# Seven of eleven column pairs of an up projection with seven combined products for eight in a quarter of their K range

## The chip, the cores and the metric

The kernel runs on one core of one Trainium2 chip. The metric is the device time of one launch in microseconds (us), as the median of several runs. One more execution was recorded by the hardware profiler; its page and its trace are what is read here. The engines are named as in the profile: PE is TensorE's matmul, PEld its weight load, DVE is VectorE, ACT is ScalarE, POOL is GpSimd, SP is SyncE. POOL and SP do little but issue transfers here.

## The reference

One decoder layer for 256 tokens of width 2048. The part that the change touches is the gated MLP at its end:

```python
h = rms_norm(x, ln2[l])
u = causal_dwconv(h @ w_up[l], ffn_conv[l], ffn_conv_bias[l])
u_gate, u_val = jnp.split(u, 2, axis=-1)
x = x + (jax.nn.silu(u_gate) * u_val) @ w_down[l]
```

`w_up` is 2048 x 11264: 5632 gate columns and 5632 value columns. `w_down` is 5632 x 2048.

## The kernel before

**Products of three.** All large products take fp32 inputs apart into a high part in the fp32r format and a low part, the rest. ACT casts the high part, DVE subtracts it from the source (`split`, lines 104 and 101 of the profile), and TensorE multiplies high by high, high by low and low by high (`main_mm`, line 93). The weights come as raw blocks of 128 x 2048 fp32, 1 MB each (`fetch`, line 116), into `wraw`, which has four buffers; POOL's queue asks for those of the MLP. A block is split in two halves of 1024 columns. The parts go to a ring of four places (`wh` and `wl`), so a half can be cast when TensorE has finished with the half four before it.

**The up projection** (`ps_up`) takes 22 column blocks of 512 columns, a gate block and then its value block, so 11 column pairs. K has 16 blocks of 128 rows. `by_token` works through one column block with four raw blocks; a raw block holds four K-blocks. The activations `h2`, high and low, are the stationary side (128 x 128), the weights the moving side (128 x 512). A column block has two token halves, two PSUM banks, and 16 x 2 x 3 = 96 products, a pair 192, the projection 2112. A half of 1024 columns holds two K-blocks and feeds 12 products.

**Behind each column block** ACT scales the two banks into `ut` (line 1003), and `convolved` runs in the background: DVE transposes 32 x 32 blocks (line 470), 16 small transfers of SP's queue put the blocks in place (`uc<-xt`, line 475), and after a pause four channels follow one by one, each a scaled copy on ACT (line 956), two steps on DVE (line 958), and for a value block the product with the gate (line 975) into `acts`. The gate block ends with a Silu (line 980). The background advances by one step for every eight wide products (`tick`, `EVERY`); `wait(12)` is the pause of twelve steps between the transfers and the convolution. Another background task turns the residual `x1` in four parts (`residual_turned`).

**The down projection** (`pd`) follows without a break, on the same ring with three more places. Some of its blocks already use seven combined products for eight (`seven`, `folds`): DVE adds quarters of the raw block (line 1049), and sums on PSUM are put together at the end (lines 1075 to 1083).

**What sets the order.** Each engine executes its own list in order. The tile framework puts the lists together while the program is built, from the order in the code, priorities and `issue_after`; which instruction stands before which can be listed from the built program. A wait of one instruction holds everything behind it on that engine.

## Time and profile before

| | |
|---|---|
| Median of three runs | 1395.56 us (1395.29 to 1396.97) |
| Profiled execution | 1401.47 us, span 1399.7 us |
| Up projection, first to last product | 696.3 to 1161.8 us |
| Busy in the span | PE 1386.3, PEld 1203.2, DVE 1036.1, ACT 794.3, POOL 128.5 us |
| Mean granted TensorE clock | 0.997 of full speed |

The profile gives, for each group of instructions, the line, the engine, the operation, what it writes and reads by the program's names, how often, the busy time and the mean duration, then the idle time of the engine before it and what ended that. `wl<-wraw,wh` is a low part on DVE, `wh<-wraw` a cast on ACT, `ah` and `al` are the parts of the activations of the down projection. Products on TensorE overlap, so the distance of their starts tells more than their duration. In the views by window, the columns are the busy microseconds and the number of instructions of each engine, the granted clock, the busy share of the DMA engines and GB/s.

### The profile page before, as it was taken

Reading aid. Unit: us, or ns where it says so; the run is one execution under the profiler, and the core shown is the slowest. Engines: PE = TensorE matmul, PEld = TensorE weight load, DVE = VectorE, ACT = ScalarE, POOL = GpSimd, SP = SyncE. Lnnn points to the kernel's source line nnn. Section 1 sums busy time; section 2 is a strip of 40 time slices with the busy share of each in tenths; the row PEclk is TensorE's granted clock in tenths of the full one; section 3 lists DMA queues with packets and bytes.
Section 4 is the critical chain, followed back from the end, with each engine's and each line's share of the span. In section 5 each row is a group of like instructions: output and inputs, shape, how many; then the busy total and the mean of one; then the engine's idle time right before and its main releaser. Section 6 shows DMA issues by size and latency. Waiting matters only on the chain.

```text
span 1399.7 us, 19586 instructions
## 1 busy us (share of the span) xinstructions
PE 1386.3 (99%) x7222; PEld 1203.2 (86%) x7222; DVE 1036.1 (74%) x1544; ACT 794.3 (57%) x987; POOL 128.5 (9%) x204
## 2 busy tenths in 40 slices
PE   9999999999999999999999999999999999999997
PEld 8998899888888888889888888888888888888886
DVE  7988886987664446767757676676676676999994
ACT  6765455645466544445546555555555566666763
POOL 0021000200001100001201011010110110101110
PEclk9999999999999999999999999999999999999999
DMA  9566554567546555776567888888888777556562
GB/s 366 182 214 214 210 197 132 189 194 262 197 133 214 210 189 183 243 260 216 192 209 223 241 218 236 237 222 235 230 227 235 220 227 229 200 186 231 179 246 72
DMA packets 204672, 297.40 MB, mean 212 GB/s; under 512 B 167096, under 2 KB 169536, under 8 KB 172064
## 3 DMA queue, kind: packets, MB, share of 16 engines
q1 hardware_dynamic: 165648, 150.31, 35.5%
q0 software_dynamic: 21088, 142.17, 29.8%
q10 hardware_dynamic: 17840, 3.67, 1.3%
q8 instruction: 56, 0.92, 0.3%
q14 instruction: 40, 0.33, 0.1%
HBM read 273.48 MB, written 3.15 MB: 198 GB/s over the span
## 4 chain that ended last, share of the span: by engine, by line
PE 95%; DMA 3%; DVE 1%; issue 0%; SPq 0%; ACT 0%; DVEq 0%; ACTq 0%
PE ps_up L93 33%; PE pd L93 14%; PE ps_gate L93 11%; PE ps_gdn L93 9%; PE ps_wo L93 6%; PE ps_br L93 6%; PE ps_moba L93 5%; PE ps_v L93 3%; PE ps_z L93 3%; DMA uc<-xt 1%; PE g L81 1%; PE ps_gdn L262 1%; DMA dT<-X 0%; DMA xs<-in_xw 0%; DMA TL<-dT 0%
## 5 line engine op out<-in xcount | busy, mean ns | idle before, releaser
L101 DVE TENSOR_TENSOR wl<-wraw,wh 128x1024 fp32r<-128x1024 f32 (+1 forms) x476 | 576.1, 1215 | 288.7 <-ACT wh L104 282.5
L104 ACT CAST wh<-wraw 128x1024 fp32r<-128x1024 f32 (+1 forms) x476 | 491.7, 1038 | 457.3 <-PE ps_up L93 168.2
L93 PE MATMUL ps_up<-wh,h 128*128 128x512 f32 x1408 | 422.8, 380 | 0.2 <-DVE x L918 0.2
L93 PEld LDWEIGHTS ps_up<-wh,h 128*128 128x128 f32 x1408 | 264.2, 188 | 46.0 <-issue 0.6
L93 PE MATMUL ps_up<-wl,h 128*128 128x512 f32 x704 | 267.6, 380 | 0.0
L93 PE MATMUL ps_gate<-wh,hc 128*128 128x512 f32 x512 | 155.4, 382 | 0.0
L93 PEld LDWEIGHTS ps_up<-wl,h 128*128 128x128 f32 x704 | 132.2, 188 | 22.7
L93 PE MATMUL ps_gdn<-hc,wh 128*128 128x256 f32 x720 | 124.2, 276 | 0.0
L93 PEld LDWEIGHTS ps_gate<-wh,hc 128*128 128x128 f32 x512 | 95.8, 188 | 16.3
L93 PEld LDWEIGHTS ps_gdn<-hc,wh 128*128 128x128 f32 x720 | 108.5, 188 | 1.3 <-issue 0.6
L93 PE MATMUL ps_gate<-wl,hc 128*128 128x512 f32 x256 | 97.9, 383 | 0.0
L93 PE MATMUL ps_gdn<-hc,wl 128*128 128x256 f32 x360 | 97.9, 275 | 0.0
L93 PE MATMUL ps_wo<-mc,wh 128*128 128x512 f32 x256 | 85.6, 379 | 0.0
L116 POOL DMA_DIRECT2D wraw<-in_w_up x88 | 46.9, 532 | 413.7 <-DVE wl L101 413.7
L93 PE MATMUL pd<-tt,ah 128*128 128x512 f32 x282 | 82.6, 381 | 0.0
L93 PE MATMUL ps_moba<-wh,hc 128*128 128x512 f32 x256 | 77.1, 381 | 0.0
L93 PE MATMUL ps_wo<-mc,wl 128*128 128x256 f32 x256 | 70.5, 276 | 0.0
L93 PEld LDWEIGHTS ps_gdn<-hc,wl 128*128 128x128 f32 x360 | 67.1, 188 | 0.3
L104 ACT CAST tt<-wraw 128x1024 fp32r<-128x1024 f32 x46 | 47.4, 1045 | 30.7 <-PE pd L93 25.0
L93 PE MATMUL pd<-wh,ah 128*128 128x512 f32 x156 | 59.7, 384 | 1.7 <-ACT ah L104 1.7
L93 PEld LDWEIGHTS pd<-tt,ah 128*128 128x128 f32 x282 | 53.2, 189 | 9.3
L93 PE MATMUL pd<-wh,al 128*128 128x512 f32 x156 | 59.3, 385 | 0.7 <-DVE al L101 0.7
(445 smaller groups left out, 1980.4 us busy)
## 6 DMA issues: line engine op xcount, KB each, us to landing
wraw<-in_w_up POOLq DMA_DIRECT2D x88, 1024.0 KB, 5.7
wraw<-in_w_dn POOLq DMA_DIRECT2D x44, 1024.0 KB, 5.9
wraw<-in_w_gate SPq DMA_DIRECT2D x32, 1024.0 KB, 4.9
wraw<-in_w_gdn SPq DMA_DIRECT2D x22, 1024.0 KB, 4.9
wraw<-in_w_moba SPq DMA_DIRECT2D x16, 1024.0 KB, 6.2
wraw<-in_w_o SPq DMA_DIRECT2D x16, 1024.0 KB, 5.7
uc<-xt SPq DMA_DIRECT2D x352, 32.0 KB, 4.6
wraw<-in_w_z SPq DMA_DIRECT2D x8, 1024.0 KB, 7.1
```

What stands on the lines that cost most here:

```text
L81: pe.matmul(ps, a, b, start=(start and i == 0), stop=(stop and i == n - 1), **kw)
L93: r = pe.matmul(ps, a, b, start=start, stop=stop, skip_group_check=True)
L101: return (eng or dve).tensor_tensor(lo, src, hi.bitcast(F32), op=ALU.subtract)
L104: casts.append(act.copy(hi, src))
L116: fetcher[0].dma_start(raw[:, :n], src)
L262: pe.matmul(ps_q0[:, b], wq[:, j, b * P:(b + 1) * P], xs[:, j], start=(j == b == 0), stop=False, skip_group_check=True)
```

## The change

The column pairs 1 to 7 (`UPS`) take their first four K-blocks together: with the two token halves, the two column blocks (gate and value) and two groups of two K-blocks, the first quarter of K is a 2 x 2 by 2 x 2 block product. Instead of eight block products of six matmuls, `fewer` does seven of six (Strassen's scheme in Winograd's form): 42 matmuls for 48.

- Four combinations of the activations are built once, in the background of the first pair (`combinations`, `forms`).
- For each changed pair, DVE makes four sums over the raw blocks (`t1`, `r11`, `t2` twice), seven halves are split where four were, ACT copies the first product out of PSUM (`m1`), and DVE folds five sums of 512 columns (`fold_v`, `fold_y`, and three that are written back to PSUM).
- Six of the seven stand ahead of the gate block's other three raw blocks; the seventh (`rest`) and the last two folds stand behind them. The background takes no step while the six are put out (`paused`).
- The host puts the first quarter of gate and value columns into two raw blocks by K-block (`up_blocks`). The first lies in a `wraw` buffer as before; the second is asked for by the code a column block earlier and lies in a part of `acts` that is still free (`spare(28, 8)`). In POOL's list of the built program its fetch stands directly behind the first's.
- All pairs run through `one_side`, with four PSUM banks to a pair instead of two to a column block; pairs take turns on all eight banks (`four_banks`).
- Background buffers: `xt` has two buffers, which the residual's turning shares; the gate `sgt` has one instead of two. The last column block's pause is 15 steps instead of 12.

```diff
+UPS = (1, 2, 3, 4, 5, 6, 7)
...
-    spent = [0]
+    spent, paused = [0], [False]
...
-        if spent[0] >= EVERY:
+        if spent[0] >= EVERY and not paused[0]:
...
-    def fetch(src, n=2048):
-        raw = wpool.tile([P, 2048], F32, name="wraw", tag="wraw", bufs=4)
-        fetcher[0].dma_start(raw[:, :n], src)
-        return raw
+    def fetch(src, raw=None):
+        if raw is None:
+            raw = wpool.tile([P, 2048], F32, name="wraw", tag="wraw", bufs=4)
+        fetcher[0].dma_start(raw, src)
+        return [raw[:, 1024 * h:1024 * h + 1024] for h in range(2)]
...
-    turned_ring = [3]
+    turned_ring = [(3 + len(UPS)) % 4]
...
-                        ub.tile([P, 8, P], F32, name="xt"), sp, 4, 1)
-        yield from wait(12)
+                        ub.tile([P, 8, P], F32, name="xt", bufs=2), sp, 4, 1)
+        yield from wait(12 if n < NF // 2 - 1 else 15)
         if not val:
-            gates[c] = ub.tile([P, 4, T], F32, name="sgt", bufs=2)
...
+    forms = [[b.tile([P, 2 * T + 64], F32R, name=t, tag=t)[:, 8:8 + 2 * T] for t in ("ah", "al")] for _ in range(2)]
+
+    def combinations():
+        raw = acts[:, 40:44, :]
+        sums = acts[:, 36:40, :].rearrange("p k t -> p (k t)").rearrange("p (f j t) -> p f j t", f=4, t=P)
+        for k in range(4):
+            act.activation(raw[:, k, :], x1[:, k, :], AF.Identity, scale=ln2v[:, k:k + 1])
+        a11, a12, a21, a22 = (raw[:, e::2, i * P:i * P + P] for i in range(2) for e in range(2))
+        s7, s5, s6, s3 = (sums[:, n] for n in range(4))
+        yield
+        dve.tensor_tensor(s7, a11, a21, op=ALU.subtract)
+        dve.tensor_tensor(s5, a21, a22, op=ALU.subtract)
+        yield
+        dve.tensor_tensor(s6, a22, s7, op=ALU.add)
+        dve.tensor_tensor(s3, a12, s6, op=ALU.subtract)
+        for n, (hi, lo) in enumerate(forms):
+            yield
+            split(hi, lo, sums[:, 2 * n:2 * n + 2].rearrange("p f j t -> p (f j t)"))
+
+    def part(src):
+        w = parts(60)
+        lows.append(split(*w, src))
+        return w
+
+    def products(w, them):
+        for bank, a, n, start in them:
+            for y_, x_ in ((0, 0), (0, 1), (1, 0)):
+                main_mm(fours(bank), a[x_], fours(half(w[y_], n, 512)), start and y_ + x_ == 0, False)
+
...
+    def fewer(ps, raw1, raw2):
+        c11, c12, c21, c22 = ps
+        fold_v, fold_y = spare(40, 2), spare(42, 2)
+
+        def of(k, i):
+            return [h_of(k + 2 * j, i) for j in range(2)]
+
+        def pair_of(bank, a, w, start=False):
+            products(w, [(bank, a[j], j, start and j == 0) for j in range(2)])
+
+        s7, s5, s6, s3 = ([combined(n, j) for j in range(2)] for n in range(4))
+
+        def add(to, one, other, op=ALU.add):
+            dve.tensor_tensor(to, one, other, op=op)
+
+        (r10, r11), (r20, r21) = raw1, raw2
+        t1 = ub.tile([P, 1024], F32, name="t1")
+        t2 = spare(36, 4)
+        add(t1, r10, r11)
+        add(r11, r11, r21)
+        add(t2, t1, r21)
+        pair_of(c11, of(0, 0), part(r10), True)
+        m1 = b.tile([P, 4 * P], F32, name="m1", tag="S", bufs=1)
+        act.copy(m1, c11)
+        pair_of(c22, s6, part(t2), True)
+        add(fold_v, c22, m1, ALU.subtract)
+        pair_of(c21, s7, part(r11), True)
+        add(t2, t2, r20)
+        add(fold_y, c21, fold_v, ALU.subtract)
+        add(c21, c21, fold_v, ALU.subtract)
+        pair_of(c12, s5, part(t1), True)
+        pair_of(c11, of(1, 0), part(r20))
+        pair_of(c21, of(1, 1), part(t2))
+
+        def rest():
+            with tc.issue_after(lows[-1].ins):
+                add(c22, c12, fold_y, ALU.subtract)
+                add(c12, c12, fold_v)
+            pair_of(c12, s3, part(r21))
+
+        return rest
+
+    def one_side(ps, c, side, q0, to=4):
+        for q in range(q0, to):
+            raw = fetch(w_up[8 * c + 4 * side + q])
+            for h in range(2):
+                w = part(raw[h])
+                k = 4 * q + 2 * h
+                products(w, [(ps[2 * i + side], h_of(k + n, i), n, k + n == 0) for i in range(2) for n in range(2)])
+
+    def spare(ch, n):
+        return acts[:, ch:ch + n, :].rearrange("p k t -> p (k t)")
+
...
+    def four_banks(name):
+        turned[0] ^= 1
+        t = [mmt(name).rearrange("p a b -> p (a b)") for _ in range(4 if turned[0] else 2)]
+        return [t[n] for n in (0, 2, 1, 3)] if turned[0] else [sdt(name) for _ in range(2)] + t
+
+    bg.append(combinations())
+    bg.append(residual_turned())
+    for c in range(NU):
+        ps = four_banks("ps_up")
+        rest = None
+        if c in UPS:
+            paused[0] = True
+            rest = fewer(ps, fetch(w_up[8 * c]), second)
+            paused[0] = False
+        one_side(ps, c, 0, c in UPS)
+        evicted(c, ps, 0)
+        if rest:
+            rest()
+        if c + 1 in UPS:
+            second = fetch(w_up[8 * c + 12], spare(28, 8))
+        one_side(ps, c, 1, c in UPS, 4 - (c == NU - 1))
+        if c < NU - 1:
+            evicted(c, ps, 1)
+    pd = four_banks("pd")
+    banks = [[0, 1, 2, 3], [4, 5, 6, 7]]
+    residual_in(0)
+    one_side(ps, NU - 1, 1, 3)
+    evicted(NU - 1, ps, 1)
+    pd += four_banks("pd")
...
+    def up_blocks(w):
+        w = w.reshape(KD, P, 2, NF // 4, 512).transpose(3, 1, 0, 2, 4)
+        w = np.stack([w[:, :, k:k + 4, n] for n in range(2) for k in range(0, KD, 4)], axis=1)
+        for c in UPS:
+            w[c, [0, 4]] = np.stack([np.concatenate([w[c, n, :, e::2] for n in (0, 4)], axis=1) for e in range(2)])
+        return w.reshape(-1, P, 2048)
```

**On TensorE**, where a new pair begins: a number behind a name is a buffer's. Before, the first raw block of a column block:

```order
L93 MATMUL ps_up_6905<-wh_61,h2_5401 128x4x32x4 x2
L93 MATMUL ps_up_6905<-wl_62,h2_5401 128x4x32x4
L93 MATMUL ps_up_6905<-wh_61,h2_5401 128x4x32x4 x2
L93 MATMUL ps_up_6905<-wl_62,h2_5401 128x4x32x4
L93 MATMUL ps_up_6906<-wh_61,h2_5401 128x4x32x4 x2
L93 MATMUL ps_up_6906<-wl_62,h2_5401 128x4x32x4
```

Now, the first two of the seven combined products of pair 2 (6760 and 6763 are two of its banks; `ah_6145` and `al_6146` are a combination of the activations):

```order
L94 MATMUL ps_up_6760<-wh_61,h2_5401 128x4x32x4 x2
L94 MATMUL ps_up_6760<-wl_62,h2_5401 128x4x32x4
L94 MATMUL ps_up_6760<-wh_61,h2_5401 128x4x32x4 x2
L94 MATMUL ps_up_6760<-wl_62,h2_5401 128x4x32x4
L94 MATMUL ps_up_6763<-wh_61,ah_6145 128x4x32x4
L94 MATMUL ps_up_6763<-wh_61,al_6146 128x4x32x4
L94 MATMUL ps_up_6763<-wl_62,ah_6145 128x4x32x4
L94 MATMUL ps_up_6763<-wh_61,ah_6145 128x4x32x4
L94 MATMUL ps_up_6763<-wh_61,al_6146 128x4x32x4
L94 MATMUL ps_up_6763<-wl_62,ah_6145 128x4x32x4
```

A split half now serves one bank with six products, where it served two banks with twelve.

**On DVE**, at the same place. Before, low parts of two raw blocks with the convolution between them:

```order
L101 TENSOR_TENSOR wl_62<-wraw_8033,wh_61 128x1024
L975 TENSOR_TENSOR acts_6142<-sgt_7820,cvf_8014 128x256
L958 SCALAR_TENSOR_TENSOR cvf_8028<-uc_7751,ffv_5500,cvf_8028 128x255
L958 SCALAR_TENSOR_TENSOR cvf_8028<-uc_7751,ffv_5500,cvf_8028 128x254
L101 TENSOR_TENSOR wl_62<-wraw_8033,wh_61 128x1024
L975 TENSOR_TENSOR acts_6142<-sgt_7820,cvf_8028 128x256
L101 TENSOR_TENSOR wl_62<-wraw_8069,wh_61 128x1024 x2
```

Now, pair 5 from its third split half (`wraw_7783`, r11) to the first half of the next raw block (`wraw_7843`); L1037 are the new sums and folds:

```order
L1037 TENSOR_TENSOR acts_6142<-acts_6142 128x1024
L102 TENSOR_TENSOR wl_62<-wraw_7783,wh_61 128x1024
L102 TENSOR_TENSOR wl_62<-t1_7785,wh_61 128x1024
L102 TENSOR_TENSOR wl_62<-acts_6142,wh_61 128x1024
L1037 TENSOR_TENSOR acts_6142<-ps_up_7780,m1_7797 128x512
L102 TENSOR_TENSOR wl_62<-acts_6142,wh_61 128x1024
L1037 TENSOR_TENSOR acts_6142<-ps_up_7779,acts_6142 128x512
L1037 TENSOR_TENSOR ps_up_7779<-ps_up_7779,acts_6142 128x512
L102 TENSOR_TENSOR wl_62<-wraw_7843,wh_61 128x1024
L960 SCALAR_TENSOR_TENSOR cvf_7849<-uc_7514,ffv_5500,cvf_7849 128x255
L472 STREAM_TRANSPOSE xt_7855<-ut_7776 128x1024
L960 SCALAR_TENSOR_TENSOR cvf_7865<-uc_7514,ffv_5500,cvf_7865 128x255
```

The first fold stands behind the fifth low part, the other two behind the sixth; the folds read PSUM.

**On ACT**, some five blocks into the down projection, where the last value block is convolved (`cvf` from `uc_9735` before, `uc_9823` now; `tt` and `wh` are weights, `ah` activations). Before:

```order
L104 CAST ah_9886<-acts_6142 128x512
L104 CAST tt_9716<-wraw_9963 128x1024
L956 ACTIVATE cvf_9954<-uc_9735,ffv_5500 128x256
L104 CAST tt_9716<-wraw_9963 128x1024
L956 ACTIVATE cvf_9977<-uc_9735,ffv_5500 128x256
L104 CAST wh_61<-wraw_10012 128x512
L104 CAST ah_9920<-acts_6142 128x512
```

Now:

```order
L105 CAST ah_9979<-acts_6142 128x512
L105 CAST tt_9809<-wraw_10051 128x1024 x2
L958 ACTIVATE cvf_10076<-uc_9823,ffv_5500 128x256
L105 CAST wh_61<-wraw_10090 128x512
L105 CAST ah_10013<-acts_6142 128x512
L105 CAST wh_61<-wraw_10090 128x1024
```

One cast moved ahead of the first `cvf`, and the second `cvf` moved behind the next `ah`.

More of the change, by code (lines that the diff above doesn't have):

```diff
@@ L131, in load_w @@
             w[h] = into[h] or parts(o, ol)
-            lows.append(split(*w[h], raw[:, 1024 * h:1024 * h + 1024]))
+            lows.append(split(*w[h], raw[h]))
         return w
@@ L157, in mmt @@
     def mmt(name):
-        return pst[0].tile([P, 2, 2, T] if wide[0] is True else [P, 2, T], F32, name=name, tag="mm")
+        return pst[0].tile([P, 2, 2, T] if wide[0] else [P, 2, T], F32, name=name, tag="mm")
     def sdt(name):
@@ L192, in by_token @@
     def by_token(ws, x, kt, name):
-        if wide[0] is True:
+        if wide[0]:
             t = mmt(name)
@@ L950, in residual_turned @@
             blk = x1[:, 4 * q_:4 * q_ + 4, :].rearrange("p k t -> p (k t)")
-            yield from turn(r3(blk, P), blk, ub.tile([P, 8, P], F32, name="xr"), act, 1, 3)
+            yield from turn(r3(blk, P), blk, ub.tile([P, 8, P], F32, name="xt", bufs=2), act, 1, 3)
     def conv3(t, u, ch):
@@ L965, in convolved @@
         yield from turn(r3(uc.rearrange("p k t -> p (k t)"), P), ut.rearrange("p k i c -> p (k i c)"),
-                        ub.tile([P, 8, P], F32, name="xt"), sp, 4, 1)
-        yield from wait(12)
+                        ub.tile([P, 8, P], F32, name="xt", bufs=2), sp, 4, 1)
+        yield from wait(12 if n < NF // 2 - 1 else 15)
         if not val:
-            gates[c] = ub.tile([P, 4, T], F32, name="sgt", bufs=2)
+            gates[c] = ub.tile([P, 4, T], F32, name="sgt")
         for k in range(4):
@@ L980, in convolved @@
             act.activation(gates[c], gates[c], AF.Silu)
-    bg.append(residual_turned())
+    NU = NF // 4
     fetcher[0] = pool
-    pd = [None] * 8
-    banks = [[2, 3, 6, 7], [0, 1, 4, 5]]
-    def accumulators(n):
-        for i in range(2):
-            pd[n + i] = mmt("pd").rearrange("p a b -> p (a b)")
-    def residual_in(p, i):
-        for h in range(2):
-            n = 2 * p + h
-            act.copy(r3(pd[banks[p][2 * i + h]], P), x1[:, 4 * n:4 * n + 4, i * P:i * P + P])
-    for n in range(NF // 2):
-        if n == NF // 2 - 1:
-            accumulators(2)
-            residual_in(0, 0)
-        ps = by_token(w_up[4 * ((n % 2) * 11 + n // 2):][:4], h2, KD, "ps_up")
+    forms = [[b.tile([P, 2 * T + 64], F32R, name=t, tag=t)[:, 8:8 + 2 * T] for t in ("ah", "al")] for _ in range(2)]
@@ new lines, in half, with h_of, combined @@
+    def half(t, n, w=1024):
+        return t[:, n * w:(n + 1) * w]
+    def part(src):
[6 more added lines that the diff above has]
+                main_mm(fours(bank), a[x_], fours(half(w[y_], n, 512)), start and y_ + x_ == 0, False)
+    def h_of(k, i):
+        return [h2[:, k, x_, i * P:i * P + P] for x_ in range(2)]
+    def combined(n, j):
+        return [t[:, (n % 2 * 2 + j) * P:(n % 2 * 2 + j + 1) * P] for t in forms[n // 2]]
@@ L1001, in layer_kernel, with evicted @@
+    def one_side(ps, c, side, q0, to=4):
[7 more added lines that the diff above has]
+        return acts[:, ch:ch + n, :].rearrange("p k t -> p (k t)")
+    def evicted(c, ps, n):
         ut = ub.tile([P, 4, 2, P], F32, name="ut", bufs=2)
@@ L1002, in layer_kernel @@
         for i in range(2):
-            act.activation(ut[:, :, i, :], r3(ps[i], P), AF.Identity, scale=R2c[:, i:i + 1])
-        bg.append(convolved(n, ut))
-    accumulators(6)
-    residual_in(0, 1)
-    accumulators(4)
-    pd[:2] = sdt("pd"), sdt("pd")
+            act.activation(ut[:, :, i, :], r3(ps[2 * i + n], P), AF.Identity, scale=R2c[:, i:i + 1])
+        bg.append(convolved(2 * c + n, ut))
+    turned = [0]
+    def four_banks(name):
+        turned[0] ^= 1
+        t = [mmt(name).rearrange("p a b -> p (a b)") for _ in range(4 if turned[0] else 2)]
+        return [t[n] for n in (0, 2, 1, 3)] if turned[0] else [sdt(name) for _ in range(2)] + t
@@ new lines, in residual_in @@
+    def residual_in(p):
+        for j in range(4):
+            n = 2 * p + j % 2
+            act.copy(r3(pd[banks[p][j]], P), x1[:, 4 * n:4 * n + 4, j // 2 * P:(j // 2 + 1) * P])
+    bg.append(combinations())
[16 more added lines that the diff above has]
+            evicted(c, ps, 1)
@@ L1045, in seven @@
         b1 = [t[:, :512] for t in b1]
-        lows.append(split(*b1, blk(raw, 0)))
-        lows.append(split(*b2, raw[:, 1024:]))
+        lows.append(split(*b1, blk(raw[0], 0)))
+        lows.append(split(*b2, raw[1]))
+        r4 = [blk(r, n) for r in raw for n in range(2)]
         for to, more in ((0, 1), (1, 3), (3, 0), (2, 3)):
-            dve.tensor_tensor(blk(raw, to), blk(raw, to), blk(raw, more), op=ALU.add)
+            dve.tensor_tensor(r4[to], r4[to], r4[more], op=ALU.add)
         with tc.issue_after(lows[-1].ins):
@@ L1054, in seven @@
         split(*s_, S)
-        split(*t13, raw[:, :1024])
-        split(*t42, raw[:, 1024:])
+        split(*t13, raw[0])
+        split(*t42, raw[1])
         def prod(bank, x_, nx, y_, ny, own=False):
@@ L1113, in layer_kernel @@
             for h in range(2):
-                lows.append(split(*w[h], blk(raw, h, 1024)))
+                lows.append(split(*w[h], raw[h]))
             if last:
```

7 lines of the change are left out of this document (3 added, 4 removed).

## The prediction

> **What bounds the kernel now.** I read the page first (sections 1 and 4), then the windows around the up projection, then the groups of one stage by engine, then single instructions in the timeline.
>
> ```profile
> PE 1386.3 (99%) x7222; PEld 1203.2 (86%) x7222; DVE 1036.1 (74%) x1544; ACT 794.3 (57%) x987; POOL 128.5 (9%) x204
> PE 95%; DMA 3%; DVE 1%; issue 0%; SPq 0%; ACT 0%; DVEq 0%; ACTq 0%
> ```
>
> TensorE is busy for 99% of the span and carries 95% of the chain that ended last; the up projection (ps_up) is 33% of that chain. Its own rows, from the view by tile (minimum/median/maximum ns, first and last start):
>
> ```profile
> L93 PE MATMUL ps_up<-wh,h x1408: 380/380/467, 696.3 to 1161.5; 128*128 128x512 f32 x176
> L93 PE MATMUL ps_up<-wl,h x704: 380/380/398, 696.8 to 1161.8; 128*128 128x512 f32 x176
> ```
>
> 2112 products start between 696.3 and 1161.8, one every 0.220 us (465.5/2111). The 380 ns are latency, since the products overlap; what a removed product gives back is 0.220 us. The waits of TensorE in the same stretch, and four windows (busy us of PE, PEld, DVE, ACT, POOL), two in the up projection and two in the down projection:
>
> ```profile
> PE ps_up L93 <- DVE x L918: 0.2, 1, 0.2
> ...
> 800.00:850.00 50.00, 50.00 (x229) 42.66 (x228) 35.29 (x44) 29.27 (x35) 5.30 (x10) 1.00 0.81 223
> 850.00:900.00 50.00, 50.00 (x229) 42.65 (x228) 36.38 (x52) 29.10 (x35) 4.77 (x9) 1.00 0.88 239
> 1200.00:1250.00 50.00, 50.00 (x229) 42.66 (x228) 49.70 (x70) 32.57 (x42) 5.31 (x10) 1.00 0.61 215
> 1300.00:1350.00 50.00, 50.00 (x229) 42.66 (x228) 49.19 (x69) 31.92 (x41) 5.31 (x10) 1.00 0.58 211
> ```
>
> In the up projection TensorE has no wait, the clock is full, and DVE is the next engine at 71 to 73%. In the down projection DVE stands at 98 to 99% and TensorE still loses nothing there. So a removed product counts in full for as long as DVE can feed the rest, and the question is DVE's budget per column pair.
>
> **The products.** A pair takes 192 products, 192 x 0.220 = 42.24 us. With seven combinations of 6 products for 48, a changed pair takes 186, or 40.92 us. Seven pairs: 42 x 0.220 = 9.24 us less.
>
> **DVE's budget.** Its groups in eight undisturbed pairs of before (busy us and mean ns | idle before it):
>
> ```profile
> L101 DVE TENSOR_TENSOR wl<-wraw,wh 128x1024 fp32r<-128x1024 f32 x129 | 157.6, 1222 | 101.7 <-ACT wh L104 101.7
> L470 DVE STREAM_TRANSPOSE xt<-ut 128x1024 f32<-128x1024 f32 x16 | 19.8, 1237 | 0.0
> L958 DVE SCALAR_TENSOR_TENSOR cvf<-uc,ffv,cvf 128x254 f32<-128x254 f32 x32 | 14.6, 478 | 0.3
> L975 DVE TENSOR_TENSOR acts<-sgt,cvf 128x256 f32<-128x256 f32 x32 | 13.4, 420 | 0.3
> ```
>
> A mean is not yet what an instruction costs a full queue; the starts tell that:
>
> ```profile
> 811.61 0.48 DVE L958 SCALAR_TENSOR_TENSOR cvf<-uc,ffv,cvf 128x254 f32<-128x254 f32 x1
> 812.00 0.42 DVE L975 TENSOR_TENSOR acts<-sgt,cvf 128x256 f32<-128x256 f32 x1
> 812.34 1.22 DVE L101 TENSOR_TENSOR wl<-wraw,wh 128x1024 fp32r<-128x1024 f32 x1
> 813.47 0.42 DVE L975 TENSOR_TENSOR acts<-sgt,cvf 128x256 f32<-128x256 f32 x1
> ...
> 1242.55 0.68 DVE L101 TENSOR_TENSOR tt<-S,tt 128x512 fp32r<-128x512 f32 x1
> 1243.15 1.22 DVE L101 TENSOR_TENSOR tt<-wraw,tt 128x1024 fp32r<-128x1024 f32 x1
> ```
>
> Each starts about 0.09 us before its forerunner ends: a low part costs 1.13 (812.34 to 813.47), a convolution step 0.39, a gate product 0.34, an operation on 512 columns 0.60. A pair before: 16 low parts 18.1, two transposes 2.3, 16 convolution steps 6.2, four gate products 1.4; together 28.0 of 42.24.
>
> The order of the changed kernel adds, per changed pair: three low parts (seven combined halves are split where four were), four sums of 1024 columns and five folds of 512 columns that read or write PSUM. The nearest rows (a plain f32 sum of 1024 columns, and sums on PSUM in the down projection):
>
> ```profile
> L303 DVE TENSOR_TENSOR sq<-sq,sq x1: 1218/1218/1218, 19.7 to 19.7; 128x1024 f32<-128x1024 f32 x1
> L1079 DVE TENSOR_TENSOR fu<-pd,fv 128x512 f32<-128x512 f32 x2 | 1.4, 688 | 0.0
> L1083 DVE TENSOR_TENSOR pd<-pd,fu 128x512 f32<-128x512 f32 x2 | 1.4, 696 | 0.3 <-PE pd L93 0.3
> ```
>
> At 1.13 and 0.60 that is 7 x 1.13 + 5 x 0.60 = 10.9, so 38.9 of 40.92 us: 95%, below the 98 to 99% of the down projection. On the mean DVE holds, with 2 us to spare per pair; three of the changed pairs also hold a residual transpose (1.15).
>
> **The stretch of the seven products** is tighter than the mean. A combined half feeds only 6 products (1.32 us) instead of 12 (2.64), and the ring has four places. ACT's casts and the copy of the first product:
>
> ```profile
> L104 ACT CAST wh<-wraw 128x1024 fp32r<-128x1024 f32 x129 | 135.2, 1048 | 125.5 <-PE ps_up L93 124.6
> L1074 ACT COPY m<-pd x2: 574/575/576, 1256.1 to 1352.9; 128x512 f32<-128x512 f32 x2
> ```
>
> Take the start of the first product as 0. The fifth half (r20) needs the place freed at 1.32: cast to 2.5, low part to 3.7. Then DVE's queue has the first fold (to 4.3), the sixth half's low part (to 5.45; ACT did the copy first, so its cast ends near 4.2), and two more folds, the last of which writes the bank that the sixth half adds to: 6.65, visible at 6.75. TensorE is there at 5 x 1.32 = 6.60. It waits 0.15 to 0.2 us. The next half follows at 7.9 against 8.1, the one after it (behind a transpose and two steps) at 11.0 against 10.8, where the low part is only read by the third product. So these two are on time, barely. No row shows the hand-overs between three engines in this form. Lower end 0 (the down projection's windows), upper end one cast, 1.05 per pair. I take 0.4, nearer to the windows, whose combinations have the same shape: 7 x 0.4 = 2.8 us.
>
> **Transfers.** The bytes stay the same. POOL asks for a pair's first block when the block four before it is split, and for the second raw block directly behind. Landing times from issue (min/median/max), in the up projection and for two fetches 1.1 us apart in the down projection:
>
> ```profile
> DMA to landing us min/median/max: 5.1/5.7/7.2
> ...
> DMA to landing us min/median/max: 5.2/6.4/7.6
> ```
>
> In DVE's order the first sum stands three low parts behind the split that frees the first block's buffer; there DVE keeps step with TensorE, 2.64 us per half, so the sum comes some 6.4 to 7.9 us after the issue. The second block is needed two or three DVE steps on, near 10 us. That is just covered, and a late block first eats the split halves that TensorE has ahead. Cost 0.
>
> **What hides the rest.** ACT gets three casts and a copy per pair (3.7 us), with some 18 us idle per pair (the 125.5 us before casts, over eight pairs, are 15.7 of them). The combinations of the activations are built once in the first pair, which stays at 28.0 of 42.24 on DVE. Held-back background steps run in the rest of the pair. The single gate buffer waits for nothing, since in DVE's order a gate's convolution already follows the last use of the gate before. Two banks per side are evicted while four others fill.
>
> **The end of the up projection.** TensorE's largest wait after the first half of the program lies 26 us into the down projection:
>
> ```profile
> 1187.16 0.60 ACT L956 ACTIVATE cvf<-uc,ffv 128x256 f32<-128x256 f32 x1 [7.78 <-DMA uc<-xt]
> 1187.67 1.03 ACT L104 CAST tt<-wraw 128x1024 fp32r<-128x1024 f32 x1
> 1188.61 0.60 ACT L956 ACTIVATE cvf<-uc,ffv 128x256 f32<-128x256 f32 x1
> 1189.11 0.60 ACT L104 CAST wh<-wraw 128x512 fp32r<-128x512 f32 x1
> 1189.62 0.62 ACT L104 CAST ah<-acts 128x512 fp32r<-128x512 f32 x1
> ...
> 1188.18 0.39 PE L93 MATMUL pd<-wh,al 128*128 128x512 f32 x1
> 1190.29 0.49 PE L93 MATMUL pd<-wh,ah 128*128 128x512 f32 x1 [1.72 <-ACT ah L104]
> ...
> 1191.95 0.49 PE L93 MATMUL pd<-wh,al 128*128 128x512 f32 x1 [0.71 <-DVE al L101]
> ```
>
> ACT stands for 7.78 us before the last block's convolution, whose turned data are late, and the cast ah that TensorE needs queues behind it. The starts show 1.9 and some 0.9 us lost. The changed order (a wait of 15 for 12) puts one cast and one convolution step less between that landing and ah: ah comes 1.03 + 0.5 = 1.5 us sooner, al some 1.9 sooner. If the landing keeps its place, TensorE loses about 1.0 instead of 2.8: 1.8 gained, ends 0 and 2.8.
>
> **Sum.** -9.24 + 2.8 - 1.8 = -8.2 us on an execution of 1401.47 us (span 1399.7); I carry it to the median of the runs, 1395.56, which lies 0.4% lower: **1387.4 us**.
>
> **Rivals.**
> *Feeding eats most of it.* Lateness in the tight stretch or of the two close fetches costs 1 us per pair instead of 0.4, and the end gives nothing: -9.24 + 7 = -2.2, 1393. For it: the 0.2 us of margin above, and three engines in one ring. Against it: the down projection does the like at 99% DVE without a wait.
>
> *DVE becomes the bound, and it ends slower.* If the new DVE work takes its whole duration, a changed pair needs 23 x 1.22 + 5 x 0.69 + 2 x 1.24 + 16 x 0.475 + 4 x 0.42 = 43.3 us against TensorE's 40.92. The queue loses 2.4 per pair, 16.8 in seven, less one lead of 5.6 (three halves of 2.64, less a cast and a low part). With 2.8 from the stretch and 1.0 gained at the end: -9.24 + 16.8 - 5.6 + 2.8 - 1.0 = +3.8, 1399. It decides from about 42.2 us of DVE per pair. Against it stand the starts 1.13 apart. The Trainium skill, "VectorE: DVE Perf Modes", section "The DRAIN you can't avoid", says that the next operation does not start until the pipeline has emptied. By that rule the whole durations count and this rival's time would come; the trace disagrees, with 1.13 between starts for a 1.22 us instruction.
>
> *The end wait goes entirely and the stretch costs nothing:* -9.24 - 2.8 = -12.0, 1383.5.
>
> **How the numbers follow.** The forecast (1385 to 1390.5) gets 0.60, the better end 0.08, feeding eats most 0.22 (1390.5 to 1396), DVE as the bound or another late hand-over beyond zero 0.10. The measurement tells about 0.2%, 2.8 us: faster means below 1392.8. Of the third case 0.12 is below that and 0.10 within 0.2% of before: faster 0.80, same 0.10, slower 0.10. The range runs from the best end, 1383.2, to 1394.
>
> **What would show it.** The ps_up products 2070 instead of 2112, spaced 0.220, and the stage some 6 us or more shorter. DVE at 90 to 97% in the changed pairs. TensorE's waits in ps_up, 0.2 us before, below 4 us in total and on DVE's fold of the third bank or on low parts. The wait on ah at the start of the down projection near 1 us. The prediction is wrong if ps_up waits for low parts in every pair by more than 1 us, if a DVE sum waits for a raw block's transfer, or if the wait on ah grows.

## The result and the profile after: slower, on transfers that the prediction gave no price

The changed kernel takes 1416.29 us (median of four runs, 1413.78 to 1422.57) against 1396.13 for the kernel before on the same chip: ratio 1.0147, interval [1.0125, 1.0168], so some 20 us slower. The forecast was 1387.4, its range ended at 1394.0. Ratios and intervals, here and in the table of runs, leave out one execution each of e3, e8 and e12 that took far longer than the rest (1436.55, 2390.84 and 3919.53 us). The profiled execution is the longest of the four (1422.57 us, span 1420.8, granted clock 0.994).

The page's busy times and its chain that ended last:

```profile
PE 1388.0 (98%) x7180; PEld 1195.0 (84%) x7180; DVE 1110.6 (78%) x1634; ACT 814.5 (57%) x1021; POOL 128.2 (9%) x204
PE 69%; DMA 18%; SPq 4%; DVE 4%; issue 3%; ACT 1%; DVEq 0%; ACTq 0%
DMA uc<-xt 17%; PE pd L94 15%; PE ps_gate L94 12%; PE ps_gdn L94 9%; PE ps_wo L94 6%; PE ps_moba L94 6%; PE ps_br L94 6%; PE ps_up L94 6%; SPq L477 4%; PE ps_v L94 3%; PE ps_z L94 3%; DVE wl L102 1%; DVE xt L472 1%; DMA x<-xt 1%; DVE cvf L960 1%
```

TensorE has its 42 products less, but its share of the chain falls from 95% to 69%. What took its place is `uc<-xt`, the small transfers that turn a column block behind its products. `ps_up` carries 6% of the chain where it had 33%. The view by tile and three windows of the up projection (busy us of PE, PEld, DVE, ACT, POOL, then clock, DMA share, GB/s):

```profile
L94 PE MATMUL ps_up<-wh,h x1268: 380/380/628, 695.2 to 1183.0; 128*128 128x512 f32 x182
L94 PE MATMUL ps_up<-wl,h x634: 380/380/792, 695.6 to 1183.2; 128*128 128x512 f32 x159
...
783.00:824.00 41.00, 39.75 (x177) 32.66 (x176) 36.01 (x45) 25.18 (x32) 4.23 (x8) 1.00 0.71 210
906.00:947.00 41.00, 39.03 (x175) 32.29 (x174) 39.62 (x51) 24.86 (x31) 4.23 (x8) 1.00 0.81 230
1029.00:1071.00 42.00, 37.32 (x156) 30.75 (x155) 27.42 (x41) 20.77 (x27) 3.18 (x6) 0.92 0.71 195
```

2070 products run from 695.2 to 1183.2. That is 488.0 us where 2069 x 0.220 would be 455.2: 32.8 us lost, against 1.0 before. This number, the *loss in ps_up*, is used below for every run. DVE is not full: 88% and 97% in the first two windows. The last window holds the end of pair 7 and the first half of pair 8, which is not a changed pair, and it is the worst: DVE has 27.4 us of work in 42 and TensorE stands 4.7. Not all of that loss is waiting. The granted clock is 0.92 there; the stretch around the end of the longest wait, by itself, has 0.50:

```profile
1063.60:1070.30 6.70, 5.32 (x13) 4.16 (x14) 6.63 (x12) 3.73 (x6) 0.53 (x1) 0.50 0.46 96
```

Products start 0.43 us apart in it instead of 0.22, which makes some 2.5 of the 32.8 us.

The waits (us in total, times, longest) and the landing times of the small transfers (min/median/max), these of after and then of before:

```profile
PE ps_up L94 <- DVE wl L102: 13.7, 15, 3.8
DVE xt L472 <- DMA uc<-xt: 32.4, 9, 8.4
ACT cvf L958 <- DMA uc<-xt: 27.0, 9, 5.5
ACT sgt L958 <- DMA uc<-xt: 13.5, 2, 8.5
```

```profile
DMA to landing us min/median/max: 1.9/5.3/12.1
```

```profile
DMA to landing us min/median/max: 1.9/4.6/10.0
```

TensorE waits for low parts. ACT and DVE, which make them, stand before data that are being turned: ACT before a convolution, DVE before a transpose. One such place, in the timeline:

```profile
1062.42 0.60 ACT L958 ACTIVATE sgt<-uc,ffv 128x256 f32<-128x256 f32 x1 [8.51 <-DMA uc<-xt]
1062.57 1.25 DVE L472 STREAM_TRANSPOSE xt<-ut 128x1024 f32<-128x1024 f32 x1 [8.40 <-DMA uc<-xt]
1062.92 1.03 ACT L105 CAST wh<-wraw 128x1024 fp32r<-128x1024 f32 x1
1063.74 1.18 DVE L102 TENSOR_TENSOR wl<-wraw,wh 128x1024 fp32r<-128x1024 f32 x1
1064.98 0.79 PE L94 MATMUL ps_up<-wl,h 128*128 128x512 f32 x1 [3.78 <-DVE wl L102]
```

Both engines wait over 8 us for the same block. The cast behind ACT's wait, the low part behind DVE's and the product behind both are late in turn. Why are the turned data late? At another place, in pair 2, the transfers start six microseconds after their transpose. Before, with the next start on SP, and now:

```profile
784.02 1.24 DVE L470 STREAM_TRANSPOSE xt<-ut 128x1024 f32<-128x1024 f32 x1
...
785.29 65.25 SPq L475 DMA_DIRECT2D uc<-xt  x51
```

```profile
791.55 1.24 DVE L472 STREAM_TRANSPOSE xt<-ut 128x1024 f32<-128x1024 f32 x1
...
796.87 0.87 DVE L960 SCALAR_TENSOR_TENSOR cvf<-uc,ffv,cvf 128x254 f32<-128x254 f32 x2
...
797.80 2.97 SPq L477 DMA_DIRECT2D uc<-xt  x4
```

Before the change the first transfer started 1.3 us after each of the 22 transposes. Here SP starts the moment the convolution steps that read `uc` have ended (796.87 + 0.87 = 797.74), and these belong to the block two before, in the same one of two `uc` buffers. The code says why: a block's background takes 21 steps (1 transpose, 4 of transfers, 12 of pause, 4 channels). A pair had 24 of them. With the steps held back for 36 products (`paused`) it has some 19 (150/8 = 18.75), so the block after next wants the buffer before the chain is through.

### The profile page after: what moved, and what is told of

It reads as the page before. It is cut to its first block, busy times and chain, and to the rows that moved or that the text cites. A ratio compares the mean times of both kernels' runs of the same rounds, so it can differ in the third digit from the quotient of the medians.

```text
span 1420.8 us, 19701 instructions
## 1 busy us (share of the span) xinstructions
PE 1388.0 (98%) x7180; PEld 1195.0 (84%) x7180; DVE 1110.6 (78%) x1634; ACT 814.5 (57%) x1021; POOL 128.2 (9%) x204
## 4 chain that ended last, share of the span: by engine, by line
PE 69%; DMA 18%; SPq 4%; DVE 4%; issue 3%; ACT 1%; DVEq 0%; ACTq 0%
DMA uc<-xt 17%; PE pd L94 15%; PE ps_gate L94 12%; PE ps_gdn L94 9%; PE ps_wo L94 6%; PE ps_moba L94 6%; PE ps_br L94 6%; PE ps_up L94 6%; SPq L477 4%; PE ps_v L94 3%; PE ps_z L94 3%; DVE wl L102 1%; DVE xt L472 1%; DMA x<-xt 1%; DVE cvf L960 1%
## 5 line engine op out<-in xcount | busy, mean ns | idle before, releaser
L102 DVE TENSOR_TENSOR wl<-wraw,wh 128x1024 fp32r<-128x1024 f32 x462 | 556.5, 1213 | 192.5 <-ACT wh L105 188.3
L105 ACT CAST wh<-wraw 128x1024 fp32r<-128x1024 f32 x462 | 475.3, 1036 | 376.6 <-PE ps_up L94 85.3
L94 PE MATMUL ps_up<-wh,h 128*128 128x512 f32 x1268 | 375.9, 383 | 7.0 <-DVE ps_up L1037 5.7
L94 PEld LDWEIGHTS ps_up<-wh,h 128*128 128x128 f32 x1268 | 238.3, 189 | 51.8 <-DVE ps_up L1037 8.3
L94 PE MATMUL ps_up<-wl,h 128*128 128x512 f32 x634 | 234.1, 384 | 9.5 <-DVE wl L102 9.5
L94 PEld LDWEIGHTS ps_up<-wl,h 128*128 128x128 f32 x634 | 119.7, 189 | 34.9 <-DVE wl L102 14.2
L118 POOL DMA_DIRECT2D wraw<-in_w_up x81 | 43.0, 530 | 425.7 <-DVE wl L102 419.3
L94 PEld LDWEIGHTS pd<-tt,ah 128*128 128x128 f32 x282 | 53.8, 191 | 12.1 <-ACT ah L105 2.7
L94 PE MATMUL pd<-wl,ah 128*128 128x512 f32 x156 | 59.1, 380 | 0.0
```

The source lines that it names most:

```text
L94: r = pe.matmul(ps, a, b, start=start, stop=stop, skip_group_check=True)
L102: return (eng or dve).tensor_tensor(lo, src, hi.bitcast(F32), op=ALU.subtract)
L105: casts.append(act.copy(hi, src))
L118: fetcher[0].dma_start(raw, src)
```

## The experiments

Four theories. **A**: a block's chain of steps no longer fits into a pair; the two `uc` buffers hold up its transfers. **B**: DVE's work and the hand-overs in the seven products starve TensorE by themselves. **C**: raw blocks now come in bunches (four asked for within 9 us) and slow the small transfers. **D**: the residual's turning shares `xt`, holds one of its two buffers for some 100 us at a time, and the blocks have one left. The table shows medians, ratios to the kernel before, the loss in ps_up, and the *tail*: span less the last ps_up product, which is 233.2 us where nothing waits.

| run | median us | ratio, interval | loss in ps_up | tail |
|---|---|---|---|---|
| before (profiled 1401.47) | 1396 | 1 | 1.0 | 237.9 |
| after | 1416.29 | 1.0147 [1.0125, 1.0168] | 32.8 | 237.6 |
| e13_t1_moved | 1418.15 | 1.0155 [1.0131, 1.0180] | 28.2 | 233.3 |
| e3_uc3 | 1394.02 | 0.9975 [0.9956, 0.9994] | 6.0 | 236.0 |
| e5_own_xr | 1403.83 | 1.0057 [1.0029, 1.0085] | 14.8 | 233.2 |
| e8_uc3_late_residual | 1392.60 | 0.9969 [0.9956, 0.9982] | 1.0 | 237.8 |
| e6_order_only | 1395.74 | 0.9995 [0.9982, 1.0007] | 1.0 | 233.2 |
| e12_order_only_held_back | 1397.54 | 1.0009 [0.9991, 1.0027] | 1.0 | 233.3 |
| e2_no_pause | 1427.16 | 1.0220 [1.0190, 1.0249] | 38.4 | 234.6 |
| e7_no_pause_own_xr | 1398.70 | 1.0008 [0.9994, 1.0023] | 13.5 | 233.2 |
| e1_wait10 | 1427.90 | 1.0219 [1.0197, 1.0242] | 31.4 | 243.9 |
| e10_uc3_wait14 | 1407.69 | 1.0075 [1.0048, 1.0102] | 22.9 | 233.3 |
| e11_uc3_residual_by2 | 1407.45 | 1.0081 [1.0063, 1.0098] | 18.6 | 235.9 |
| e14_uc3_residual_in_acts | 1392.88 | 0.9971 [0.9955, 0.9986] | 1.1 | 234.8 |
| e15_last_waits | 1397.72 | 1.0000 [0.9987, 1.0013] | 4.7 | 239.6 |
| e16_before_last_wait | 1401.84 | 1.0040 [1.0027, 1.0053] | 1.0 | 239.3 |

### A third buffer for the turned block

```diff
-        uc = ub.tile([P, 4, T], F32, name="uc", bufs=2)
+        uc = ub.tile([P, 4, T], F32, name="uc", bufs=3)
-        t1 = ub.tile([P, 1024], F32, name="t1")
+        t1 = spare(24, 4)
```

> A third buffer for uc, the turned block; to make room for it, the sum t1 lies in a part of acts that is not yet in use. The steps, the DVE work and the fetches stay. Theory A, in the form that the two uc buffers hold up the transfers: the first transfer starts 1.3 us after the transpose again instead of 6, ACT and DVE stop waiting, 1390 to 1402 us. Theory B: 1412 to 1420. Theory C: the start is early but the landing stays at 7 to 12 us, part of the loss stays, 1403 to 1414.

The loss falls from 32.8 to 6.0 us and the time to 1394.0. The same transpose as above, now with SP's next start, and TensorE's last products:

```profile
790.83 1.23 DVE L472 STREAM_TRANSPOSE xt<-ut 128x1024 f32<-128x1024 f32 x1
...
792.12 6.88 SPq L477 DMA_DIRECT2D uc<-xt  x10
...
796.15 0.86 DVE L960 SCALAR_TENSOR_TENSOR cvf<-uc,ffv,cvf 128x254 f32<-128x254 f32 x2
```

```profile
L94 PE MATMUL ps_up<-wl,h x634: 380/380/499, 695.5 to 1156.2; 128*128 128x512 f32 x159
```

The transfers start 1.3 us after the transpose again and no longer behind the steps at 796. The control moves `t1` alone:

> The changed kernel with nothing but t1 moved into acts: the control for the runs with three uc buffers and with the residual's own buffer, which both needed that room. Theories A and D: nothing hangs on it, two uc buffers and the shared xt buffers are as before, 1411 to 1422 us. If the move of t1 was what helped there: 1394 to 1405.

1418.15 us, with transfers that start 4 to 7 us after their transpose at the same blocks: the move is not what helped. Theory A is shown as the main cause: 28.2 us of loss with two buffers, 6.0 with three. The fetches come in bunches in both (single small transfers land after up to 12.9 and 11.5 us), so C by itself is not the cause.

### The residual out of the blocks' way

With two `uc` buffers and a buffer of the residual's own:

```diff
-            yield from turn(r3(blk, P), blk, ub.tile([P, 8, P], F32, name="xt", bufs=2), act, 1, 3)
+            yield from turn(r3(blk, P), blk, ub.tile([P, 8, P], F32, name="xr"), act, 1, 3)
```

> The changed kernel with its pause and two uc buffers, but the residual turns through a buffer of its own, so that the blocks have both xt buffers (t1 lies in acts, as in the run with three uc buffers, so this is also the control for that move). Theory A (the two uc buffers hold the transfers up): the first transfer of every second block still starts about 6 us after its transpose, 1408 to 1420 us. Theory D (the residual holds one xt buffer for some 100 us at a time, the blocks have one left, and a transpose waits for the transfers of the block before): DVE's waits before transposes go, 1390 to 1400 us. If the move of t1 was what helped, it is fast too, but with the late starts still there.

Between the two: 14.8 us lost. What is left of DVE's waits before the blocks' transposes is for ACT's `ut` and no longer for transfers (before a single block 3.1 us at the most):

```profile
DVE xt L472 <- ACT ut L1080: 4.4, 3, 3.1
```

The transfers still start 2 to 7 us after their transpose, instead of 1.3, in twelve blocks. So D is a cause of its own beside A: a second free `xt` halves what the late transfers cost, since one block's lateness no longer holds the next block's transpose. The two causes work on each other: the third `uc` buffer alone takes away 22.2 of the 28.2 us, the residual's own buffer alone 13.4, more than 28.2 together. Three `uc` buffers, and the residual only behind the changed pairs and at every step instead of every third:

```diff
-        yield from wait(26)
+        yield from wait(156)
-            yield from turn(r3(blk, P), blk, ub.tile([P, 8, P], F32, name="xt", bufs=2), act, 1, 3)
+            yield from turn(r3(blk, P), blk, ub.tile([P, 8, P], F32, name="xt", bufs=2), act, 1, 1)
```

> Three uc buffers with the pause, and the residual is turned only after the seven changed pairs, every step instead of every third. In the run with three uc buffers (1394.0 us) four transposes still waited 0.5 to 2.1 us and ps_up lost 6.0 us. Theory D: these waits go with the residual out of the way, ps_up loses 2 to 4 us, 1390 to 1393. Theory B: what is left is the stretch itself, ps_up loses 5 to 7 us and the time stays at 1392 to 1396. The faster turning at the end may cost there: above 1396 if its transfers delay the last blocks.

```profile
L94 PE MATMUL ps_up<-wl,h x634: 380/380/398, 695.6 to 1151.3; 128*128 128x512 f32 x159
```

```profile
824.00:865.00 41.00, 41.00 (x188) 35.00 (x187) 39.30 (x52) 27.49 (x34) 4.23 (x8) 1.00 0.79 239
906.00:947.00 41.00, 41.00 (x188) 34.97 (x187) 39.30 (x51) 27.50 (x35) 4.22 (x8) 1.00 0.79 233
```

ps_up now takes 456.2 us, 9.3 less than before, with no product late. DVE has 39.30 us of work in each window of 41, or 96%, and starves nobody. Theory B, as the cause of what the changed kernel lost, falls. The 42 saved products pay their 9.24 us in full as soon as the background's buffers keep up.

### The late transfers without the full DVE

> No pair is a changed one: all eleven do 192 products, no block is held for sums, nothing is held back; what stays of the change is the new order of the blocks and banks, the single gate buffer, the two xt buffers shared with the residual, and the 15 steps of the last block. Theories A, B and C: the rest of the change costs little, 1393 to 1398 us, as before. Theory D (sharing xt between the residual and the blocks, or the single gate buffer, is what makes the transfers late): 1402 to 1415, with waits of DVE's transposes for uc and x transfers as in the changed kernel.

With `UPS = ()` the new order, banks and buffers change nothing: 1395.74 us. Then the held-back steps alone, in that kernel:

```diff
+        if paused[0]:
+            paused[0] -= 1
-        if spent[0] >= EVERY and not paused[0]:
+        elif spent[0] >= EVERY:
...
+        paused[0] = 42 if 1 <= c <= 7 else 0
```

> No product is saved and no block is held for sums (all eleven pairs do 192 products, DVE has 28 us of work in 42), but the background steps are held back for the first 42 products of pairs 1 to 7, which leaves them the 18.75 steps per pair of the changed kernel; two uc buffers, xt shared with the residual. If late transfers alone are enough (theories A and D): they start late here too and ps_up loses 10 to 30 us, 1403 to 1425. If it takes late transfers and a DVE that is full at 96%, so that its lead cannot be won back: ps_up loses less than 5 us, 1394 to 1400, though the transfers start late.

```profile
782.78 1.24 DVE L474 STREAM_TRANSPOSE xt<-ut 128x1024 f32<-128x1024 f32 x1
...
786.16 0.48 DVE L962 SCALAR_TENSOR_TENSOR cvf<-uc,ffv,cvf 128x254 f32<-128x254 f32 x1
...
786.70 13.48 SPq L479 DMA_DIRECT2D uc<-xt  x16
```

```profile
783.00:824.00 41.00, 41.00 (x188) 34.96 (x188) 28.55 (x37) 23.66 (x29) 3.99 (x8) 1.00 0.82 234
```

The same kind of late start behind the same steps, 3.9 us after the transpose, in six such blocks; but DVE has 28.6 us of work in 41, and TensorE loses nothing. So late starts alone are not enough. What has to come on top this run does not separate. Beside the full DVE it also lacks the bunched fetches: its small transfers land after 7.9 us at the most (12.1 in the changed kernel), its starts are late by 2.7 us instead of 5, and ACT's longest wait for turned data in the up projection is 0.7 us. That a DVE at 96% cannot win back the lead that a wait costs it is an argument, not shown. Against it as the whole story, the largest loss of any pair of the changed kernel, 6.7 us, falls into pair 8, which has DVE's work of before, behind the waits of 8.51 and 8.40 us shown above. A full DVE and bunched fetches without the late starts are not enough either: the run with the late residual has both (single small transfers land after up to 11.3 us) and loses 1.0.

### The steps not held back

```diff
-            paused[0] = True
+            paused[0] = False
```

> The background steps also run during the 36 products of each changed pair where the change held them back: 23.25 steps per pair instead of 18.75, against a chain of 21. Theory A: the transfers start in time again, 1390 to 1402 us, ps_up 460 to 470 us. Theory B: the transposes and convolution steps now lie inside the tight stretch, where DVE is late already: 1416 to 1430. Theory C: the fetches are bunched as before and the landing stays long, 1410 to 1420.

Theory A's number was missed: every transfer starts in time and TensorE still loses 38.4 us.

```profile
DVE xt L472 <- DMA x<-xt: 20.7, 4, 5.8
PE ps_up L94 <- DVE wl L102: 22.4, 8, 6.2
```

DVE stands before transposes for an `xt` buffer, and TensorE for the low parts behind them. With the residual's own buffer as well:

> No pause, two uc buffers, and the residual's own buffer. Without the pause the blocks' transfers started in time and ACT never waited, and yet 38 us were lost in ps_up; the open question is to what. Theory D: DVE stood up to 5.8 us before seven of the transposes for the one xt buffer left, so these waits go and the loss in ps_up falls from 38 to under 10 us, 1388 to 1398 us. Theory B (transposes and convolution steps inside the stretch of the seven products starve it): the waits before transposes go but TensorE still waits for low parts there, 1410 to 1427 us.

No transpose waits for a transfer, and the loss falls from 38.4 to 13.5. That is D again, worth some 25 us here (`t1` moved too, which changed nothing in the control). For what stays, these waits:

```profile
PE ps_up L94 <- DVE ps_up L1037: 4.5, 4, 1.3
PE ps_up L94 <- DVE wl L102: 3.7, 6, 1.3
DVE acts L1037 <- DMA wraw<-in_w_up: 9.1, 6, 3.0
```

TensorE waits for folds and low parts in and just behind the stretch, where the background's steps now stand between them; that is B in a small form. But DVE's sums also wait for raw blocks, 9.1 us here against 0.7 in the run with the late residual. Which of the two makes the 13.5 us stays open. With the steps held back and buffers free the loss was 1.0, so holding them back is right if the buffers allow for it.

### Fewer and more steps of pause

> Only the number of background steps between a block's turning transfers and its convolution changes, 10 for 12 (the last block keeps 15), so that a block's chain of steps takes 19 instead of 21; a changed pair now has only 18.75 steps where it had 24, and the two uc buffers come round once per pair. Theory A (the chain of a turned block no longer fits into a pair, so its transfers start late behind the block two before, and ACT and DVE stand before late data): the late start of about 6 us goes, ps_up shrinks from 488 to 460 to 470 us, 1390 to 1402 us in all. Theory B (DVE's queue and the hand-overs in the seven products, by themselves, starve TensorE): the same DVE work in the same pairs, 1412 to 1420. Theory C (raw blocks fetched in bunches slow the turning transfers to 7 to 12 us of landing): the convolution comes two steps sooner to data as late as before, so it waits more: 1416 to 1430.

A's number was missed, C's was met: 1427.90 us. The first transfer of every block starts 1.3 us after its transpose, so the buffer is free in time. But the convolution comes two steps sooner and the data don't:

```profile
ACT cvf L958 <- DMA uc<-xt: 37.6, 10, 7.9
ACT sgt L958 <- DMA uc<-xt: 19.4, 4, 7.2
```

In pairs 0 to 6 the value block's last transfer lands 18 to 25 us after its transpose (16 to 20 in the kernel before). A chain that is short enough for two buffers is too short for the transfers. That the bunched raw blocks are what slows them was not tried by itself, and the number that C got right does not need them: in the kernel before the convolution stood 19 to 20 us behind the transpose, and two steps are 3.5 us (16 products at 0.220), so by this estimate even its own landings would come too late for most convolutions that stand two steps sooner. Nor is ps_up the place where this execution is longer than the changed kernel's (31.4 us lost against 32.8); that is the tail, 243.9 against 237.6 us. The Trainium skill, "DMA: Bandwidth & Descriptors", section "Rules for kernel authors", advises to issue a transfer early and to wait late; this run agrees, since a wait two steps sooner brings ACT's waits before convolutions from 40.5 to 57.0 us; and the changed kernel shows that the time between must also be paid for in destination buffers. The other direction, with three buffers:

> Three uc buffers, and two more background steps between a block's transfers and its convolution (14 for 12). Theory C in its small form (the second block of each changed pair lands 20 to 22 us after its transpose and ACT stands 0.4 to 1.3 us before it): these waits go, ps_up loses 3 to 5 us instead of 6.0, 1390 to 1393 us. If nothing hangs on them: 1392 to 1396.

A miss: 22.9 us lost, although no convolution on ACT waits for its landing any more. In the trace TensorE waits up to 2.6 us for low parts and once 2.8 for a cast, DVE up to 5.4 before a transpose, and convolution steps stand three and four in a row ahead of low parts and sums. ACT itself once stands 7.2 us behind transfers of the residual. The number of steps also decides beside which sums a block's twelve DVE instructions come to stand; that one of these is the cause was read, not isolated.

### The residual's speed and place

> As the run with three uc buffers and the late residual (1392.6 us, ps_up at the pace of its products), but the residual's transfers go out two to a step, so that it is through some 28 steps earlier and holds an xt buffer for about 16 us at a time. If the wait of 3.0 us that TensorE has at the start of the down projection comes from the transposes of the last blocks (2.2 and 2.5 us late behind the residual): it falls below 1.5 us and the time to 1389 to 1391.5. If it is the last block's own landing (19 us after its transpose): the wait stays at 2 to 3 us, 1391 to 1394.

Slower, 1407.45, and not where it was looked for. The changed pairs lose nothing; all of TensorE's waits in ps_up, but for those at its start, lie behind 1040 us, where the residual is turned:

```profile
ACT wh L105 <- DMA x<-xt: 17.3, 3, 13.1
```

These transfers are issued from ACT's own queue. Two to a step are more than land in time, and ACT stands with its casts until earlier ones have landed. One to a step, but through parts of `acts` that are free by then:

```diff
-            yield from turn(r3(blk, P), blk, ub.tile([P, 8, P], F32, name="xt", bufs=2), act, 1, 1)
+            yield from turn(r3(blk, P), blk, spare(36 + 4 * (q_ % 2), 4).rearrange("p (k t) -> p k t", t=P), act, 1, 1)
```

> As the run with three uc buffers and the residual after the seven changed pairs, one transfer to a step (1392.6 us), but the residual turns through the parts of acts that the changed pairs' sums and folds have left free by then, two in turn, so that it never takes an xt buffer from the blocks. There ps_up kept the pace of its products (loss 1.0 us), and the last pairs' transposes waited 1.8 to 2.5 us behind the residual, ACT 5.3 us before a convolution, and TensorE 3.0 us at the start of the down projection. If the shared buffer is the cause of these: the waits before transposes are gone and the time is 1388 to 1391. If the residual's transfers, which are sixteen per block on ACT's queue beside sixteen on SP's, lengthen the landing by themselves: 1391 to 1394, with ACT still standing before the last convolutions.

The waits before transposes are gone, as the shared buffer would have it, and the profiled execution takes 1388.21 us. The median is 1392.88, no better than with the shared buffer. These two are the fastest of the study, at 0.997 of the kernel before.

### Where the rest of the gain is

ps_up is 9.3 us shorter there, the medians only 3.5. Both kernels got a longer wait ahead of the last convolutions, the kernel before for its last block alone (22 steps instead of 12), the run with the residual in `acts` for its last three pairs:

```diff
-        yield from wait(12 if n < NF // 2 - 1 else 15)
+        yield from wait(12 if n < 16 else 16 if n < NF // 2 - 1 else 22)
```

> As the run with the residual turned through acts (1392.9 us), but the blocks of the last three pairs have 16 steps between transfers and convolution instead of 12, and the last block 22 instead of 15, so that ACT does not stand before their landing and no cast of the down projection queues behind it. If the wait at the start of the down projection is what the timed executions lose: no loss in the down projection's products in the trace, and the median falls by 3 to 6 us, to 1386.5 to 1390. If the missing gain lies elsewhere: 1391.5 to 1394.

> The kernel before with one number changed: the last block has 22 steps between its transfers and its convolution instead of 12. The profiled execution of the kernel before lost 4.2 us in the down projection behind that block, but it lies 5 us above the median. If that wait belongs to the slower of its executions alone: the upper ones (1398 to 1402) go and the median stays at 1395 to 1396.5. If it is in all of them, as the prediction took it: the median falls to 1391 to 1394.

Both missed. The last block's steps now stand between those of the down projection's seven products; in both traces TensorE loses about 2 us there at two places and the tail grows to 239.6 and 239.3 us. The first run also loses 3.7 us more in ps_up, all in the last pair. One of the places, in the kernel before with its longer wait:

```profile
1226.01 0.50 PE L93 MATMUL pd<-wh,ah 128*128 128x512 f32 x1 [1.66 <-ACT ah L104]
```

The second run still settles a point: its tail is 6.1 us over the undisturbed 233.2, and its median is 5.9 us over that of the kernel before. So the median of the kernel before has hardly any wait in its tail. Its undisturbed sum says the same: 694.9 + 465.5 + 233.2 + 1.8 around the span = 1395.4. By that sum the run with the late residual would take 695.1 + 456.2 + 233.2 + 1.8 = 1386.3; its profiled execution (1390.87) has a tail 4.6 longer. With the residual in acts the profiled tail is only 1.6 longer and the median is the same, so the executions that were only timed lose some 6 us at a place that no trace here shows. That stays open.

## Why the prediction was wrong, step by step

**Products, -9.24.** Right in size: 9.3 us, once nothing else is late.

**DVE's budget, 95% of a changed pair.** Right: 96% (39.30 of 41.00), and TensorE does not wait. The rival by whole durations (43.3 us per pair) is refuted by the run with the late residual, which these rows come from: DVE's 50 operations in its pair 3 last 43.1 us added up, and keep DVE busy for 39.2. The Trainium skill, "VectorE: DVE Perf Modes", section "The DRAIN you can't avoid", from which the prediction took this rival's rule, adds that a next operation that is not held starts earlier. With that addition it does not ask for whole durations to add up, and the trace, with starts some 0.09 us before the end of the operation in front, agrees.

**The stretch of seven products, 2.8.** Its lower end, 0, with the pause and free buffers; up to 13.5 us in the run where the background runs inside it. The margin of 0.15 us was the right place to worry about; with the pause it held.

**Transfers of raw blocks, 0.** Nearly right for DVE's sums, which waited 4.7 us in all on raw blocks in the changed kernel and 0.7 with late residual and three buffers. Single waits of up to 2.2 us are one of the prediction's own signs of being wrong. What these fetches do to the small transfers was not asked.

**What hides the rest, 0.** This is the step that failed, in the sentence "Held-back background steps run in the rest of the pair". It moved steps without pricing what they issue. The steps left per pair (some 19) should have been set against a block's chain (21), and the `uc` buffers (2) against the blocks under way; the sharing of `xt` with the residual, which the change brought along, was not priced either. A third `uc` buffer brings the loss in ps_up from 28.2 to 6.0 us, and the residual out of the way brings it to 1.0; that is what this step was worth. No rival named these transfers. The trace of before even had the signs: ACT stood 7.78 us before the one block that came late, in the row quoted for the end.

**The end of the up projection, -1.8.** Wrong twice. The changed kernel's tail is 237.6 us against 237.9, so nothing was gained. The last block's landing costs TensorE nothing any more (ACT waits 2.4 us before its convolution), but now ACT stands 5.0 us before that of the block ahead of it, and TensorE 2.3 us for a cast `ah` behind. And the 2.8 us came from an execution 5 us above the median; the median of before has hardly such a wait to give. The price of the wait in that execution was low, too: behind it the granted clock was 0.50 for some 3 us, so that its tail is 4.7 us longer than an undisturbed one.

So the sum of the traces reads: start -1.1, ps_up +22.5, tail -0.3, together 21.1 us of span. In ps_up 9.2 us were won and 31.8 lost.

## What to carry to other kernels

A change that takes background steps away for a while lengthens every chain that is counted in steps: compare the chain, in steps and in microseconds, with the time until its buffers come round again, before calling the moved work hidden. A late transfer can cost nothing: behind the changed pairs of the run with the late residual ACT waited up to 3.8 us for turned data and ps_up lost nothing, where waits of over 8 us cost pair 8 of the changed kernel 6.7. So how much lead the waiting engines have left must be looked for in the waits of the neighbours too. And a wait that is to be removed should first be shown to exist in the median execution, by adding up stage lengths without it.

## What was not expected of the hardware

A block's sixteen transfers of 32 KB take 11 to 13 us to issue from SP when their landing is quick, and up to 19 us in the changed kernel, where single ones landed after 12.1 us. SP itself waits for its earlier ones (before, then after):

```profile
SPq L475 <- DMA uc<-xt: 22.3, 28, 2.1
```

```profile
SPq L477 <- DMA uc<-xt: 59.6, 41, 3.8
```

Transfers issued from ACT's queue can stop ACT's arithmetic: a cast waited 13.1 us for earlier `x<-xt` transfers (two to a step).

A wait of TensorE can cost more than its length. Around the end of the wait of 3.78 us in the changed kernel the granted clock was 0.50, from 1063.6 to 1070.3 us, and behind the 1.72 and 0.71 us in the down projection of the kernel before it was 0.50 from 1192.6 to 1195.9; products started 0.43 us apart in both stretches.
